# Kernel matrices and input projection of a state-space branch: from their own PSUM pools to the pool of the token projections

## The chip, the cores and the metric

One Trainium2 chip; the program runs on one of its cores. The metric is the device time of one execution in microseconds (us). Engines are called PE (TensorE, matmuls; PEld is its weight load), DVE (VectorE), ACT (ScalarE), POOL (GpSimd) and SP (SyncE, which issues most DMAs). "q0" and "q1" below are the two halves of the query projection.

## What is computed

A decoder block on 512 tokens of width 1024: RMS norm, one input projection (`w_in`), an S5 state-space branch and a sliding-window attention branch side by side, gates, an output projection, then a PEER mixer (128 experts for each token out of 16384). Only the front of it matters here:

```python
xn = rms_norm(h, ln1_g[layer])
proj = xn @ w_in[layer]
u_s5, q, k, v, gate_logits = jnp.split(proj, splits, axis=-1)
...
# s5_mixer: from the parameters alone
abar = exp(lam * step);  bbar = coef * b
# from the parameters and u_s5
h_t = abar * h_(t-1) + bbar @ u_t
y_t = c @ h_t + d * u_t
```

(`s5_mixer` is given here in short.) The kernel treats four tokens as one block. For that it builds from the parameters, for 16 sets of groups, a 128x128 kernel matrix `tt` of a block's inputs to its outputs, and the matrices `el` (input to state) and `f` (state to output).

## The kernel before, in words

**Pools of PSUM.** The eight banks are split in `run` (L1215 on): `psc` has two buffers with the tag "sc", `ptr` two with the tag "tr", `pmm` four with the tag "mm". A tile asks its pool for a buffer in the order in which the Python code makes the tiles, and a buffer that had an earlier tile is handed on when that tile's last reader is done.

**Token projections.** `proj_tok` takes all four buffers of `pmm` (tiles `tps`, one for each 128 tokens) and runs for k/v, q0 and q1 in turn: 96 matmuls each, three (L94, L95, L96) for every product, since each weight is split by ACT into `hi` (L124) and by DVE or POOL into `lo` (L125). The query tiles are read by ACT twice: `qt` (L549), which a DMA writes out as `q_d` (L553), and `sq` (L550), which has one buffer and is reduced by DVE into `ssq` (L551).

**Projection of the state space's input.** `proj_u` runs four times: 24 matmuls into one tile `ups` (L491, before the change from `psc`), then `ut` (L495, DVE), then copies into `up` (L500, DVE and ACT). Gate tiles `gps` come from `psc` too.

**The state space's parameters.** `s5_params` makes, on DVE and POOL, long rows of small complex products (L281 to L288) and a chain of squarings (L281 to L288 on 128x16, then L331 to L336; twelve instructions, called a turn below), whose results POOL turns into the tables `co` and `si`. Four times it then transposes two tables (`wtr`, L417, from `ptr`; read by ACT as `el`, L418), spreads a table into two tiles `wrep` (L422, ACT, one buffer each), runs eight matmuls into a tile `kps` (L419 and L426, before the change from `ptr`), and takes `kps` out in four additions by DVE (L432) and three copies by ACT (L434), which go to the same tile `tt` in turn. `s5_mix` then starts with the matmuls `eps` (L449, from `pmm`).

**Order.** `front` weaves the Python steps of the projections (k/v, q0, q1, `proj_u`) with those of `s5_params`. What each engine runs, and in which order, is then set by a scheduler which simulates the pools, engines and waits with its own costs. Each engine runs its own row of instructions in that order, so an instruction which waits holds all that stand behind it.

Of the kernel before, what the change touches and what calls it, by code (L numbers as in the profile page):

```python
# [10 lines left out]
F32 = mybir.dt.float32  # L11
# [8 lines left out]
T = 512  # L20
# [38 lines left out]
class Builder:  # L59
# [230 lines left out]
    def s5_params(self, P, tp, res):  # L290
# [107 lines left out]
        for gh in range(2):  # L398
            G = slice(8 * gh, 8 * gh + 8)
            bc = lambda a: a[:, G, None].to_broadcast(sh)  # L400
            fr, fi, cre, cim = f_re[:, G], f_im[:, G], c_re[:, G], c_im[:, G]
            self.cmul(tp, bb_re, bb_im, bc(cr), bc(ci), b_re[:, G], b_im[:, G], sh, "b")
            for t, src, k in ((w_re, bb_re, 3), (w_im, bb_im, 3), (fr, cre, 0), (fi, cim, 0)):
                for o, s in halves(t, k):
                    nc.scalar.copy(o, src[s])
            for k in (1, 2, 3):
                self.cmul(tp, halves(w_re, 3 - k), halves(w_im, 3 - k), bc(ar[k]), bc(ai[k]), bb_re, bb_im, sh, "b")
            yield 6.0
            for k in (1, 2, 3, 4):
                self.cmul(tp, halves(fr, k), halves(fi, k), bc(ar[k]), bc(ai[k]), cre, cim, sh, "f", nc.gpsimd)  # L410
            yield 4.0
            for g0 in range(0, 8, 4):
                GG = slice(8 * gh + g0, 8 * gh + g0 + 4)
                for src, dst in ((w_re, el[0]), (w_im, el[1])):
                    ps = self.ptr.tile([128, 4, 128], F32, tag="tr", name=self.nm("wtr"))
                    for g in range(4):
                        nc.tensor.transpose(ps[:, g, :], src[:, g0 + g].rearrange("p s g c -> p (s g c)"), self.ident)  # L417
                    nc.scalar.copy(dst[:, GG, :], ps)  # L418
                ps = self.ptr.tile([128, 4, 128], F32, tag="tr", name=self.nm("kps"))  # L419
                wr = [tp.tile([128, 4, 4, 32], F32, tag=f"wrep{i}", name=self.nm("wrep")) for i in range(2)]  # L420
                for i, (w, sign) in enumerate(((w_re, 1.0), (w_im, -1.0))):
                    nc.scalar.activation(wr[i], w[:, g0:g0 + 4, 3:4].rearrange("p a s g c -> p a s (g c)").to_broadcast(  # L422
                        [128, 4, 4, 32]), AF.Copy, scale=sign)
                for g in range(4):
                    for i, f in enumerate((fr, fi)):
                        nc.tensor.matmul(ps[:, g, :], wr[i][:, g].rearrange("p s c -> p (s c)"),  # L426
                                         f[:, g0 + g, 0:4].rearrange("p s g c -> p (s g c)"), start=(i == 0), stop=(i == 1))
                di = tp.tile([128, 4, 32], F32, tag="di", name=self.nm("di"))
                nc.vector.tensor_mul(di, i4[:, None, :].to_broadcast([128, 4, 32]), dsk[:, GG, None].to_broadcast([128, 4, 32]))
                for s in range(4):  # L430
                    q = slice(32 * s, 32 * s + 32)
                    nc.vector.tensor_add(tt[q, GG, 32 * s:32 * s + 32], ps[q, :, 0:32], di[q])  # L432
                    if s < 3:
                        nc.scalar.copy(tt[q, GG, 32 * s + 32:128], ps[q, :, 32:128 - 32 * s])  # L434
                yield 2.0
# [51 lines left out]
    def proj_u(self, xh, xl, up):  # L487
        nc = self.nc
        for kk in range(4):
            wh, wl = self.unit_cols(self.i["w_in"], kk * 128, 128)  # L490
            ps = self.psc.tile([128, T], F32, tag="sc", name=self.nm("ups"))  # L491
            for k in range(KD):
                self.mm3(ps, wh[:, k, :], wl[:, k, :], xh[:, k, :], xl[:, k, :], k == 0, k == KD - 1)
            ut = self.ep.tile([128, T], F32, tag="e2", name=self.nm("ut"), bufs=1)
            nc.vector.tensor_mul(ut, ps, self.rb)  # L495
            v = ut.rearrange("p (n s) -> p s n", s=4)
            for q in range(4):
                for s in range(4):
                    cp = nc.scalar.copy if s % 2 else nc.vector.tensor_copy
                    cp(up[32 * s:32 * s + 32, 4 * kk + q, :], v[32 * q:32 * q + 32, s, :])  # L500
            yield 5.2
# [982 lines left out]
```

## Time and profile before

| | |
|---|---|
| median of 3 runs | 1680.63 us (1680.52 to 1682.4) |
| the profiled execution | 1685.87 us, its span 1684.1 us |
| mean granted clock of TensorE | 0.988 |
| PE busy | 1616.7 us, 96% of the span |
| DVE busy | 1417.1 us, 84% |
| ACT busy | 836.0 us, 50% |
| POOL busy | 529.9 us, 31% |

The profile follows one execution. Its times count from the start of the span. A line such as `[3.55 <-DVE tt L432]` behind an instruction says that its engine sat idle for 3.55 us before it and that the last thing to come was DVE's instruction on `tt` at L432. All that the change names lies between 59 and 150 us, within the first tenth of the span.

### The profile page before, as it was taken

To read this page: it belongs to the slowest core of one execution; us is meant where nothing else is said; L and a number is where in the kernel's file an instruction comes from. 1 tells how busy PE (TensorE), PEld (TensorE's weight loads), DVE (VectorE), ACT (ScalarE), POOL (GpSimd) and SP (SyncE) were. 2 spreads that over 40 slices of the span, in tenths; PEclk is the share of its full clock that TensorE was granted. 3 is DMA by queue.
4 is the path that set the end of the run, shared out by engine and by line. 5 is a ranking of instruction groups with operands and counts; after the bars stand their busy time and mean duration, and the time that the engine had idled before them with its cause. 6 is when DMAs were issued, how large, how long until landed. Compare 5 with 4: busy or idle time off the path is not lost.

```text
span 1684.1 us, 25275 instructions
## 1 busy us (share of the span) xinstructions
PE 1616.7 (96%) x8831; PEld 1422.9 (84%) x8831; DVE 1417.1 (84%) x2931; ACT 836.0 (50%) x1290; POOL 529.9 (31%) x472
## 2 busy tenths in 40 slices
PE   7799999998999999999999999999999999999998
PEld 5577887786899999999999999888888887888887
DVE  7699868897797899999998976878788777878895
ACT  5256566565555346675776863333333333333332
POOL 2564022332631222222222223333333333343330
PEclk9899999999999999999999999999999999999999
DMA  7823352645764666877876989999999999999994
GB/s 233 157 88 95 113 181 92 196 139 159 222 183 138 213 241 239 302 275 254 292 271 235 342 304 348 316 335 341 328 358 343 330 345 333 340 343 354 330 361 155
DMA packets 236880, 430.42 MB, mean 256 GB/s; under 512 B 17440, under 2 KB 153680, under 8 KB 233680
## 3 DMA queue, kind: packets, MB, share of 16 engines
q1 hardware_dynamic: 174752, 241.12, 42.6%
q0 software_dynamic: 36864, 134.23, 22.6%
q10 hardware_dynamic: 25136, 53.45, 9.8%
q8 instruction: 69, 1.13, 0.3%
q14 instruction: 59, 0.48, 0.1%
HBM read 374.08 MB, written 54.66 MB: 255 GB/s over the span
## 4 chain that ended last, share of the span: by engine, by line
PE 58%; DVE 17%; DMA 5%; issue 4%; ACT 2%; POOL 0%; SPq 0%; DVEq 0%; ACTq 0%; POOLq 0%
PE po L1166 8%; PE po L1168 8%; PE po L1165 8%; PE pa L94 7%; PE pa L96 7%; PE pa L95 7%; DVE lo L125 4%; DMA v_a<-A_d 3%; DVE sp_row L1215 2%; PE pg L1092 1%; ACT hi L124 1%; PE pg L1093 1%; DMA gl<-g_d 1%; DVE g_oh L1110 1%; PE qps L94 1%
## 5 line engine op out<-in xcount | busy, mean ns | idle before, releaser
L125 DVE TENSOR_TENSOR lo<-t_raw,hi 128x1024 fp32r<-128x1024 f32 x256 | 313.1, 1223 | 59.5 <-ACT hi L124 57.3
L124 ACT CAST hi<-t_raw 128x1024 fp32r<-128x1024 f32 x256 | 268.1, 1051 | 181.1 <-PE pa L95 127.2
L94 PE MATMUL pa<-x2h,hi 128*128 128x384 f32 x1024 | 347.5, 339 | 8.1 <-ACT hi L124 6.1
L96 PE MATMUL pa<-x2h,lo 128*128 128x384 f32 x1024 | 344.7, 339 | 3.2 <-DVE lo L125 3.2
L95 PE MATMUL pa<-x2l,hi 128*128 128x384 f32 x1024 | 344.2, 336 | 0.0
L1198 POOL DMA_INDIRECT sp_row<-peer_u,sp_ei x128 | 177.5, 1386 | 446.3 <-DVE sp_row L1215 401.2
L1198 POOL DMA_INDIRECT sp_row<-peer_v,sp_ei x128 | 168.0, 1312 | 332.3 <-DVE sp_acc L1217 306.4
L1166 PE MATMUL po<-lo,v_wh 128*128 128x512 f32 x768 | 264.4, 395 | 1.7 <-DVE lo L125 1.7
L1168 PE MATMUL po<-hi,v_wl 128*128 128x512 f32 x768 | 241.2, 394 | 0.0
L1165 PE MATMUL po<-hi,v_wh 128*128 128x512 f32 x768 | 238.4, 395 | 0.9 <-ACT hi L124 0.7
L1155 ACT CAST v_wh<-v_w 128x384 fp32r<-128x384 f32 x128 | 65.8, 514 | 347.3 <-DVE v_w L1154 293.9
L94 PEld LDWEIGHTS pa<-x2h,hi 128*128 128x128 f32 x1024 | 193.2, 189 | 13.1 <-ACT hi L124 8.6
L96 PEld LDWEIGHTS pa<-x2h,lo 128*128 128x128 f32 x1024 | 192.9, 189 | 5.0 <-DVE lo L125 4.5
L95 PEld LDWEIGHTS pa<-x2l,hi 128*128 128x128 f32 x1024 | 193.0, 188 | 0.9
L1166 PEld LDWEIGHTS po<-lo,v_wh 128*128 128x128 f32 x768 | 143.6, 187 | 36.8 <-DVE lo L125 2.9
L1165 PEld LDWEIGHTS po<-hi,v_wh 128*128 128x128 f32 x768 | 143.4, 187 | 36.1 <-ACT hi L124 2.5
L1168 PEld LDWEIGHTS po<-hi,v_wl 128*128 128x128 f32 x768 | 143.9, 187 | 35.4
L1217 DVE SCALAR_TENSOR_TENSOR sp_acc<-sp_row,sp_a,sp_acc 128x1024 f32<-128x1024 f32 x128 | 163.9, 1280 | 0.4
L1215 DVE SCALAR_TENSOR_TENSOR sp_row<-sp_row,xrow 128x1024 f32<-128x1024 f32 x128 | 156.0, 1219 | 4.6 <-DMA sp_row<-peer_u,sp_ei 4.5
L124 ACT CAST hi<-raw 128x1024 fp32r<-128x1024 f32 x88 | 92.0, 1048 | 86.2 <-PE gps L95 15.6
L125 POOL TENSOR_TENSOR lo<-raw,hi 128x1024 fp32r<-128x1024 f32 x28 | 68.8, 2458 | 118.8 <-ACT hi L124 118.7
L1108 ACT COPY g_one<-g_o 128x1024 f16<-128x1024 f16 x48 | 99.1, 2065 | 7.7 <-DVE g_o L1107 5.3
(457 smaller groups left out, 2985.8 us busy)
## 6 DMA issues: line engine op xcount, KB each, us to landing
t_raw<-peer_uT SPq DMA_DIRECT2D x128, 512.0 KB, 4.6
t_raw<-peer_v SPq DMA_DIRECT2D x128, 512.0 KB, 7.0
G_d<-g_st ACTq DMA_DIRECT2D x24, 1024.0 KB, 6.4
v_g<-G_d SPq DMA_DIRECT2D x64, 384.0 KB, 9.4
raw<-w_in SPq DMA_DIRECT2D x32, 512.0 KB, 4.4
A_d<-u_g ACTq DMA_DIRECT2D x70, 192.0 KB, 4.1
v_a<-A_d SPq DMA_DIRECT2D x70, 192.0 KB, 8.4
raw<-w_ab SPq DMA_DIRECT2D x64, 128.0 KB, 3.3
```

Source lines behind the costliest of these rows:

```text
L94: mm(out, lh, rh, start=first, stop=False)
L95: mm(out, lh, rl, start=False, stop=False)
L96: mm(out, ll, rh, start=False, stop=last)
L124: self.nc.scalar.copy(hi, raw)
L125: (self.nc.gpsimd if pool_lo else self.nc.vector).tensor_sub(lo, raw, r32(hi))
L1108: nc.scalar.copy(one, o1.rearrange("p b t -> p t b"))
L1165: mm(po[j][i], wh[:, c], hi[:, hs[i]], start=first, stop=False)
L1166: mm(po[j][i], wh[:, c], lo[:, hs[i]], start=False, stop=False)
L1168: mm(po[j][i], wl[:, c], hi[:, hs[i]], start=False, stop=last)
L1198: nc.gpsimd.indirect_dma_start(out=got[k], out_offset=None, in_=self.i[n], in_offset=bass.IndirectOffsetOnAxis(ap=ei[:, s:s + 1], axis=0))
L1215: nc.vector.scalar_tensor_tensor(r, r, 1.0, xrow, op0=ALU.mult, op1=ALU.mult, accum_out=av[:, s:s + 1])
L1217: nc.vector.scalar_tensor_tensor(acc, r, av[:, s:s + 1], acc, op0=ALU.mult, op1=ALU.add)
```

## The change

Two tiles come from another pool: `kps` (four of them) from `pmm` in place of `ptr`, and `ups` (four) from `pmm` in place of `psc`. Nothing else in the code differs.

```diff
-                ps = self.ptr.tile([128, 4, 128], F32, tag="tr", name=self.nm("kps"))
+                ps = self.pmm.tile([128, 4, 128], F32, tag="mm", name=self.nm("kps"))
...
-            ps = self.psc.tile([128, T], F32, tag="sc", name=self.nm("ups"))
+            ps = self.pmm.tile([128, T], F32, tag="mm", name=self.nm("ups"))
```

In the order in which the code makes its tiles, the first two of the four `kps` stand between q0's four `tps` and q1's four. The last number of a name below counts the tiles as they are made: `tps_164_708` to `tps_167_711` are q0's tiles, `kps_262_1072` and `kps_279_1160` the first two kernel matrices, `tps_299_1236` to `tps_302_1239` q1's, `kps_327_1360` and `kps_336_1424` the last two, and then `ups_357_1517` and three more. With the change all of these go through the four buffers of `pmm` in that turn. The scheduler also makes other rows of instructions from it. Three places follow.

PE where q0 ends, as the difference between the two kernels ("+" is new at this place; six rows more of `kps_262_1072` stand where the dots are):

```order
 L96 MATMUL tps_167_711<-hi_267_1096,xl_115 128x512
+L426 MATMUL kps_262_1072<-f_re_879,wrep_263_1073 128x128
+L426 MATMUL kps_262_1072<-f_im_880,wrep_264_1074 128x128
...
+L426 MATMUL kps_279_1160<-f_re_879,wrep_280_1161 128x128
 L94 MATMUL tps_299_1236<-hi_304_1242,xh_114 128x512
 L95 MATMUL tps_299_1236<-lo_305_1243,xh_114 128x512
```

The first kernel matrix, which stood behind 76 of q1's 96 matmuls, and one matmul of the second, which stood behind all of them, now stand ahead of q1's first.

DVE around the splits of the last weights for q1 and the first for `ups`, before (`rn` is part of a turn of squarings):

```order
L334 TENSOR_SCALAR rn_103_517<-rn_103_517 128x16
L125 TENSOR_TENSOR lo_342_1449<-raw_340_1446,hi_341_1448 128x1024
L335 TENSOR_TENSOR sqr_97_505<-sqr_97_505,rn_103_517 128x16
L336 TENSOR_TENSOR sqi_98_506<-sqi_98_506,rn_103_517 128x16
L281 TENSOR_TENSOR cm1_107_527<-sqr_97_505 128x16
```

and with the change:

```order
L286 TENSOR_TENSOR sqr_137_605<-cm1_139_607,cm2_140_608 128x16
L125 TENSOR_TENSOR lo_342_1449<-raw_340_1446,hi_341_1448 128x1024
L288 TENSOR_TENSOR sqi_138_606<-cm3_141_609,cm4_142_610 128x16
...
L336 TENSOR_TENSOR sqi_146_626<-sqi_146_626,rn_151_637 128x16
L125 TENSOR_TENSOR lo_361_1563<-raw_359_1560,hi_360_1562 128x1024
L551 TENSOR_REDUCE ssq_94<-sq_344_1459 128x8
```

The split `lo_342_1449` stood in the turn that makes `rn_103`; it now stands in the turn that makes `sqr_137`, five turns further on. The first `ssq` of q1 stood inside the turn that makes `sqr_129`; it now stands behind the whole turn of `sqr_145`, two turns further on, and behind the split `lo_361_1563`.

PE where q1 ends and `ups` starts, before:

```order
L96 MATMUL tps_302_1239<-hi_341_1448,xl_115 128x512
L94 MATMUL ups_357_1517<-xh_114,hi_355_1513 128x512
L95 MATMUL ups_357_1517<-xl_115,hi_355_1513 128x512
L96 MATMUL ups_357_1517<-xh_114,lo_356_1514 128x512
L94 MATMUL ups_357_1517<-xh_114,hi_355_1513 128x512
L417 MATMUL wtr_278_1154<-ident_58,w_im_893 128x128 x4
```

and with the change (`ktr` are transposes of the keys, which stood behind the state space's mixing):

```order
L96 MATMUL tps_302_1239<-hi_341_1448,xl_115 128x512
L426 MATMUL kps_327_1360<-f_re_879,wrep_328_1361 128x128
...
L577 MATMUL ktr_458_2278<-ident_58,kv_120 128x128 x4
L577 MATMUL ktr_459_2291<-ident_58,kv_120 128x128 x4
L426 MATMUL kps_336_1424<-f_re_879,wrep_337_1425 128x128
L94 MATMUL ups_357_1517<-xh_114,hi_355_1513 128x512
L95 MATMUL ups_357_1517<-xl_115,hi_355_1513 128x512
```

Three of the four `kps` now stand whole ahead of `ups`, and of the last its first matmul; before, three stood among the matmuls of `ups` and of the gates.

## Rows read from the trace of the kernel before

**Rows 1.** The page, busy time of the span by engine: us, share, instructions.

```profile
PE 1616.7 (96%) x8831; PEld 1422.9 (84%) x8831; DVE 1417.1 (84%) x2931; ACT 836.0 (50%) x1290; POOL 529.9 (31%) x472
```

**Rows 2.** The waits of PE between 60 and 151 us: what it waited for, us in total, times, the longest.

```profile
PE kps L426 <- DVE tt L432: 5.5, 3, 3.5
PE tps L94 <- ACT sq L550: 3.2, 1, 3.2
PE ups L94 <- DVE ut L495: 2.4, 1, 2.4
```

**Rows 3.** Busy time of the engines by stretch (a table by windows): after the window and its length come PE, PEld, DVE, ACT and POOL busy us with their instructions, the granted clock, the DMA share and GB/s. Behind the part that the change touches; the last row sums 16 windows from 147.74 to 460 us.

```profile
147.74:160.00 12.26, 12.26 (x64) 10.45 (x63) 11.21 (x24) 5.52 (x8) 0.14 (x2) 1.00 0.42 129
...
180.00:200.00 20.00, 20.00 (x113) 17.36 (x113) 20.00 (x38) 9.59 (x27) 2.57 (x3) 1.00 0.35 100
...
sum 312.26, PE 295.43 PEld 250.39 DVE 255.13 ACT 181.90 POOL 84.37; mean PE 18.46 PEld 15.65 DVE 15.95 ACT 11.37 POOL 5.27
```

**Rows 4.** The timeline of PE where q0 ends and q1 starts: start, us, engine, line, operation, [idle time before it and who ended it].

```profile
62.69 0.79 PE L94 MATMUL tps<-hi,xh 128*128 128x512 f32 x1 [3.19 <-ACT sq L550]
```

**Rows 5.** The timeline of ACT before the first kernel matrix.

```profile
75.86 0.69 ACT L549 ACTIVATE qt<-tps,rx 128x512 f32<-128x512 f32 x1 [11.39 <-DMA q_d<-qt]
...
79.74 0.62 ACT L422 ACTIVATE wrep<-w_im 128x512 f32<-128x512 f32 x1
```

**Rows 6.** The timeline of PE, the first matmul of the first `kps` and what follows its last, then two matmuls of the third `kps`.

```profile
93.50 0.38 PE L426 MATMUL kps<-f_re,wrep 128*128 128x128 f32 x2
...
95.28 0.60 PE L417 MATMUL wtr<-ident,w_re 128*128 128x128 f32 x4
...
130.53 0.63 PE L426 MATMUL kps<-f_re,wrep 128*128 128x128 f32 x2
130.95 0.64 PE L426 MATMUL kps<-f_im,wrep 128*128 128x128 f32 x2
```

**Rows 7.** The timeline of DVE between 83 and 104 us.

```profile
83.46 0.17 DVE L286 TENSOR_TENSOR sqr<-cm,cm 128x16 f32<-128x16 f32 x1
...
84.23 0.28 DVE L283 TENSOR_TENSOR cm<-a3r,bb_im 128x128 f32<-128x128 f32 x1
84.42 0.29 DVE L284 TENSOR_TENSOR cm<-a3i,bb_re 128x128 f32<-128x128 f32 x1
...
88.39 0.17 DVE L281 TENSOR_TENSOR cm<-sqr 128x16 f32<-128x16 f32 x1
...
89.56 1.22 DVE L125 TENSOR_TENSOR lo<-raw,hi 128x1024 fp32r<-128x1024 f32 x1
...
90.90 0.17 DVE L281 TENSOR_TENSOR cm<-sqr 128x16 f32<-128x16 f32 x1
...
94.04 0.35 DVE L281 TENSOR_TENSOR cm<-sqr 128x16 f32<-128x16 f32 x1
...
97.78 0.17 DVE L281 TENSOR_TENSOR cm<-sqr 128x16 f32<-128x16 f32 x1
...
98.61 0.57 DVE L286 TENSOR_TENSOR w_re<-cm,cm 64x128 f32<-64x128 f32 x2
...
103.32 0.67 DVE L551 TENSOR_REDUCE ssq<-sq 128x8 f32<-128x512 f32 x1
```

**Rows 8.** All instructions on `kps`: duration in ns (least, median, most), first and last start; the additions that DVE takes it out with.

```profile
L432 DVE TENSOR_TENSOR tt<-kps,di x16: 270/286/296, 98.2 to 149.3; 32x128 f32<-32x128 f32 x16
```

**Rows 9.** Busy time by stretch, columns as in rows 3, of the part in question.

```profile
78.80:91.00 12.20, 12.20 (x50) 9.59 (x51) 11.95 (x58) 5.92 (x9) 0.00 (x0) 0.87 0.22 64
91.00:104.00 13.00, 13.00 (x70) 10.99 (x69) 12.67 (x56) 5.84 (x11) 12.15 (x31) 1.00 0.54 163
104.00:117.00 13.00, 10.52 (x56) 8.38 (x54) 12.69 (x43) 7.45 (x13) 7.20 (x11) 1.00 0.28 87
```

**Rows 10.** The timeline of ACT, q1's tail.

```profile
96.31 0.57 ACT L418 COPY el<-wtr 128x512 f32<-128x512 f32 x1
...
99.63 0.68 ACT L550 ACTIVATE sq<-tps,rx 128x512 f32<-128x512 f32 x1
...
105.18 1.04 ACT L124 CAST hi<-raw 128x1024 fp32r<-128x1024 f32 x1
```

**Rows 11.** The timeline of PE, the start of `ups`, the longest waits behind it, and the first `eps`.

```profile
100.39 0.40 PE L94 MATMUL ups<-xh,hi 128*128 128x512 f32 x1
100.62 0.39 PE L95 MATMUL ups<-xl,hi 128*128 128x512 f32 x1
...
118.05 0.50 PE L94 MATMUL ups<-xh,hi 128*128 128x512 f32 x1 [2.41 <-DVE ut L495]
...
129.22 0.46 PE L426 MATMUL kps<-f_re,wrep 128*128 128x128 f32 x2 [3.55 <-DVE tt L432]
...
147.74 1.95 PE L449 MATMUL eps<-up,el 128*128 128x128 f32 x16
```

**Rows 12.** Busy time by stretch, columns as in rows 3, two stretches of 3.5 and 4 us behind two of these waits.

```profile
119.50:123.00 3.50, 3.50 (x12) 2.77 (x11) 3.42 (x7) 2.43 (x6) 3.50 (x6) 0.51 0.00 0
...
129.20:133.20 4.00, 3.98 (x21) 4.00 (x22) 3.92 (x6) 3.75 (x7) 4.00 (x7) 0.58 0.00 0
```

**Rows 13.** All instructions on `ktr`, columns as in rows 8.

```profile
L577 PE MATMUL ktr<-ident,kv x8: 270/273/273, 201.7 to 202.4; 128*128 128x128 f32 x8
```

**Rows 14.** The timeline of POOL, one instruction of the tables.

```profile
103.24 0.43 POOL L283 TENSOR_TENSOR cm<-co,sqi 128x128 f32<-128x128 f32 x1
```

## The prediction

> **What bounds the kernel now.** I read the busy times first: PE is busy 1616.7 of 1684.1 us [rows 1], so that the time is PE's work plus the holes in it, and a change in waits is worth only what PE's holes lose or gain. Next the waits of PE in the part that the change touches: between 60 and 151 us it waited 3.2 us for ACT's `sq` (q0's last tiles), 5.5 us in three pieces for `kps` to get its bank back from DVE's additions, and 2.4 us for the bank of `ups` [rows 2]. The last two groups, 7.9 us, are what other banks can take away. Then the stretches behind: from 147.74 us on, where `eps` starts, PE is busy 12.26 of 12.26 us, and so it stays over 180 to 200, where DVE is busy 20.00 of 20 as well; from there to 460 us PE idles 312.26 - 295.43 = 16.8 us in all, none of it before 220 [rows 3]. A start of `eps` that moves by some us therefore moves what follows. The question is when `eps` starts: 147.74 in the profile [rows 11].
>
> **The first step: a kernel matrix ahead of q1.** The pools hand out buffers in the order of the code, and there the first two `kps` stand before q1's four tiles. With four buffers, q1's third and fourth tile get those of the first and second `kps`, and the scheduler has put the eight matmuls of the first, and one of the second, ahead of all of q1. PE can't start them when q0 is out, but only when ACT has both `wrep`, whose last one starts at 79.74 and takes 0.62 [rows 5]: 80.4. Until now PE used this hole: q0 ended at 62.69 - 3.19 = 59.5, and q1 started at 62.69 [rows 4]. Its matmuls of that time now lie behind. What stands ahead of that `wrep` on ACT is the same in both kernels, the wait of 11.39 us for the DMA of `q_d` among it [rows 5], so I let 80.4 stand. Eight `kps` matmuls took 95.28 - 93.50 = 1.78 us at the full clock, and 0.42 us each at the lower one [rows 6]; behind a hole of 20 us I take the lower, 3.4 us, so 83.8. The second pair of `wrep` has the same two buffers, so its first tile costs 0.62 more, and q1 starts at 84.6. Its 96 matmuls at 0.23 us (the step of two in rows 11) are 22.1 us, the second `kps` 1.8, some 2 us of `wtr` and a restart at the lower clock 1 to 2 more: q1 ends at 112, if nothing else holds it. I let it end at 115, since its last matmuls wait for `lo_342` and its fourth tile for the second `kps` to be taken out. Before it ended at 100.39 [rows 11]. So 14.7 us are lost here first. The third `kps` (1.8) and the transposes `ktr` (0.8, [rows 13]) follow at once, until 117.6. Work has moved ahead of `ups` which stood among it: three `kps` and `ktr`.
>
> **The second step: the last `kps` waits for ACT, ACT for DVE.** The last `kps` stands with one matmul at the head of `ups`. It needs its `wrep` and the banks that q1's second tile had; on ACT that `wrep` stands behind the whole tail of q1: `sq` of the second tile, which waits until DVE has reduced the first one (`sq` has one buffer), then `qt`, two `el`, `sq`, `hi`, `qt`, `sq`, `wrep`. At 0.68, 0.57 and 1.04 us for `sq` (and `qt`), `el` and `hi` [rows 10], and 0.62 for `wrep` [rows 5], these nine are 0.68 x 5 + 0.57 x 2 + 1.04 + 0.62 = 6.2 us when added up, and some 0.1 less for each since ACT starts the next a bit early: 5.7 us. So it hangs on the end of the first `ssq` of q1 on DVE.
>
> DVE has no hole there (12.67 of 13 and 12.69 of 13 us busy, [rows 9]), so its time is a sum. Up to 83.46 [rows 7] nothing has moved. There it now meets the first addition of the first `kps`, which comes out at 83.8 to 84.2: a wait of 0.7. Four additions at 0.29 [rows 8] and one `di` of 0.2 come in ahead of the turn that started at 88.39, and a `lo` goes out of it: it starts at 90.4. Instructions on DVE follow each other with an overlap of 84.23 + 0.28 - 84.42 = 0.09, so a `lo` of 1.22 costs 1.13. A turn with one `lo` in it took 90.90 - 88.39 = 2.51 us while POOL was idle, and 97.78 - 94.04 = 3.74 while POOL was at work [rows 7, 9]: 1.4 and 2.6 without the `lo`. So this turn ends at 91.8. Then follow, up to the end of that `ssq`, three `lo` (3.4), four additions (1.2), twelve halves of `w_re` and `w_im` at 0.30 (3.6, the row at 98.61 holds two), eight products of 128x128 at 0.2 (1.6), `di` 0.2 and `ssq` 0.6: 10.6 us [rows 7, 8], and six turns. All six at 1.4 end at 110.8, all at 2.6 at 118.0. POOL was busy 12.15 and 7.20 of 13 us in the two stretches behind 91 us [rows 9], and it now gets its inputs sooner, as the turns come sooner; so I take a value near the upper bound, 116.5.
>
> 116.5 + 5.7 = 122.2: the last `kps` and `ups` start there, 4.6 us after PE has run out of work.
>
> **The third step: `ups` without waits.** From there PE has four `ups` and one gate tile of 24 matmuls at 0.23, 5.55 each, and 1.8 of `kps`: 29.5 us. I see no wait in it: the four `ups` have buffers that q1 and the third and fourth `kps` left long before, and DVE has only `ut`, copies and `lo` there. So the 7.9 us go, as they should, and `eps` starts at 151.7. Behind the waits of 2.41 and 3.55 us the granted clock fell to 0.51 and 0.58, the lower level of 1.2 GHz, for 3.5 and 4 us of the work that followed [rows 11, 12]: 3.5 x 0.49 = 1.7 us each. The new hole of 4.6 us is of that kind. Since its length is the least sure number here, I put in 1.1 of the 1.7. Against that, `ktr`, 0.8 us, stood behind `eps` and is done by then. In all 151.7 + 1.1 - 0.8 - 147.74 = **4.3 us later**.
>
> The table of stretches has no hole of PE from 147.74 to 220 us [rows 3], so the shift goes on. The scheduler also reorders the attention behind; no row tells me a price for that, and I give it nothing, with 3 us to either side.
>
> **Sum.** The profiled execution took 1685.87 us, 1.8 us around its span among it; + 4.3 makes 1690.2. It lies 5.2 us above the median of the runs, 1680.63, and the shift is the same for both: **1685.0 us**.
>
> **Rivals.**
> (a) *The hole behind q1 stays short.* If turns cost DVE 1.4 rather than 2.6, `ssq` ends at 110.8, `lo_342` no longer holds q1, and `ups` starts when PE is ready, at 112 + 2.6 = 114.6, or after ACT, at 116.5. Then `eps` starts at 116.5 + 29.5 = 146.0, with no lowered clock, and with the 0.8 of `ktr` the kernel gains 2.5 us, up to 4.4 if ACT is not late either: 1677.3. For it speaks that POOL idled in part of the second stretch, against it that DVE gave POOL work in each turn.
> (b) *The shift is absorbed.* The 16.8 us of PE's holes from 220 to 460 us [rows 3] may not all hang on the chain that is late; where one waits for a DMA that was issued early, 4 us vanish. Then 1680 to 1683. Against it: DVE was full for 180 to 200, and what waits there for DVE waits later.
> (c) *DVE and POOL lock each other out.* In a turn that ran beside POOL the twelve instructions took 2.6 us in place of 1.4, so 0.1 us more for each, while one POOL instruction of the tables takes 0.43 us [rows 7, 14]. If each of the twelve waited for a whole one, a turn would cost 1.4 + 12 x 0.43 = 6.6 us, and five of the six turns would add 20 us to what I count at 2.6. As only a part of the turns meets a busy POOL, I put it at 13 us, 1698. The Trainium skill, "SBUF — State Buffer", section "Who interferes with whom", says that a VectorE instruction with two SBUF inputs and a GpSimd one that reads SBUF exclude each other for the whole instruction. The rows show them slowed, yet by a quarter of that; so I leave it a small chance.
>
> (d) *The banks pay in full.* If PE loses its 7.9 us of waits [rows 2] and the order costs nothing, since what stands behind `kps` at q1 is made up before `eps`, the kernel takes 1680.63 - 7.9 = 1672.7. The change says that the banks are free by then: for `ups` they are, for the first two `kps` they aren't, since q1 comes after them in the pool and PE is short of work from 59.5 on. So this has little for it. The Trainium skill, "Perfetto Trace Analysis", section "Matmuls", has it as a rule: independent groups of matmuls should rotate through different PSUM banks, so that one group is taken out while the next runs. By that rule the waits go; the trace has them, 7.9 us, and has no row for a loss beside them.
>
> **How the numbers follow.** A run of this kernel can be told from no change from about 0.2% on, 3.4 us. My forecast has 0.52, of which a fifth falls below 3.4 us; (a) 0.18, three quarters of it faster by more than 3.4 us when the clock and the attention's order help; (b) 0.21; (c) 0.06; (d) 0.03. Together: faster 0.14 + 0.03 = 0.17, same 0.10 + 0.04 + 0.20 = 0.34, slower 0.42 + 0.01 + 0.06 = 0.49. The range leaves out (c) and (d) and reaches from (a) with half a us to spare, 1676.5, to the forecast with all six turns at 2.6 (+1.5), the full price of the clock (+0.6) and 3 us of the attention, 1690.
>
> **What would show it.** Right: PE idle from 59.5 to about 80.4, then `kps` ahead of q1; q1's end near 115; a wait of 3 to 5 us ahead of the last `kps`, put down to ACT's `wrep` or `sq`; no wait for `ut` or `tt` inside `ups`; `eps` near 152, and the same shift at 200 us. Wrong: `wrep` much sooner than 80 us since the DMA of `q_d` lands earlier; `ups` starting by 117; an order of the attention that is worth more than 3 us by itself.

## The result and the profile after

The change makes the kernel slower: 1698.1 us (median of 4 runs, 1694.94 to 1698.33) against 1681.52 for the kernel before (4 runs), a ratio of 1.009 with a 95% interval of [1.0076, 1.0103]. A second measurement (`after2` below) gave 1698.14 against 1684.04, 1.0084 [1.0069, 1.0098]. So it costs 14 to 17 us; the forecast was 4.3, with an upper end of 1690.

The profiled execution took 1694.94 us, 9.1 more than the profiled one of before, since that one lay 4 above its median and this one 3 below. The two traces are therefore compared by when things start, up to 480 us; behind that they differ by what single executions differ.

The waits of PE between 60 and 160 us, where before had [rows 2]:

```profile
PE kps L426 <- ACT wrep L422: 23.4, 4, 19.7
PE ktr L577 <- ACT el L418: 3.8, 1, 3.8
PE wtr L417 <- DVE w_re L286: 1.7, 1, 1.7
PE tps L95 <- DVE lo L125: 1.5, 1, 1.5
PE tps L94 <- DVE tt L432: 0.2, 1, 0.2
```

Before, there is one wait more in this stretch than [rows 2] and the prediction list, and it is the longest: inside q1, PE waited for a `hi` which stands on ACT behind the same wait of 11.39 us for the DMA of `q_d` [rows 5]. The row of the waits of before, and the matmul that waited:

```profile
PE tps L94 <- ACT hi L124: 7.7, 1, 7.7
```

```profile
78.79 1.90 PE L94 MATMUL tps<-hi,xh 128*128 128x512 f32 x3 [7.67 <-ACT hi L124]
```

None of the waits of before is left, neither those of the banks (7.9 us, as the change means it) nor the others (3.2 and 7.7). In their place PE waits 23.4 us for `wrep`: 19.7 ahead of q1 and 3.1 ahead of the last `kps`, with 3.8 for `ktr` between. So the hole ahead of q1 is not all new: up to 79 us PE had stood still for 10.9 us before as well, and had done only some 8 us of q1 in between.

Busy time from the end of q0 to `eps`, columns as in [rows 3], before and with the change:

```profile
59.50:147.74 88.24, 69.52 (x314) 56.45 (x314) 74.82 (x240) 48.00 (x93) 60.32 (x113) 0.88 0.41 104
59.50:159.70 100.20, 69.46 (x322) 56.66 (x322) 74.20 (x243) 48.45 (x95) 57.88 (x116) 0.83 0.37 92
```

PE is busy for 69.5 us in both, and idle for 18.7 us before and 30.7 with the change. The 12.0 us by which `eps` is late are PE's idle time.

PE's timeline with the starts that answer to [rows 4, 6, 11]:

```profile
79.42 0.77 PE L426 MATMUL kps<-f_re,wrep 128*128 128x128 f32 x2 [19.70 <-ACT wrep L422]
...
84.58 0.77 PE L94 MATMUL tps<-hi,xh 128*128 128x512 f32 x1
...
117.01 0.38 PE L426 MATMUL kps<-f_re,wrep 128*128 128x128 f32 x2
...
122.80 1.60 PE L577 MATMUL ktr<-ident,kv 128*128 128x128 f32 x8 [3.84 <-ACT el L418]
127.52 0.80 PE L426 MATMUL kps<-f_re,wrep 128*128 128x128 f32 x2 [3.12 <-ACT wrep L422]
...
159.70 1.95 PE L449 MATMUL eps<-up,el 128*128 128x128 f32 x16
```

q1 starts at 84.58 in place of 62.69, `ups` behind the row at 127.52 in place of 100.39, and `eps` at 159.70 in place of 147.74: 12.0 us late. DVE's timeline up to q1's first reduction, where before had [rows 7]: the first instruction of a turn and of the one behind it, then the first of the last turn ahead of the reduction, the six in it that took long, and what follows.

```profile
90.54 0.17 DVE L281 TENSOR_TENSOR cm<-sqr 128x16 f32<-128x16 f32 x1
...
92.04 0.17 DVE L281 TENSOR_TENSOR cm<-sqr 128x16 f32<-128x16 f32 x1
...
114.79 0.17 DVE L281 TENSOR_TENSOR cm<-sqr 128x16 f32<-128x16 f32 x1
...
114.97 0.60 DVE L283 TENSOR_TENSOR cm<-sqr,sqi 128x16 f32<-128x16 f32 x1
...
115.57 0.59 DVE L286 TENSOR_TENSOR sqr<-cm,cm 128x16 f32<-128x16 f32 x1
...
116.20 0.56 DVE L331 TENSOR_TENSOR rn<-sqr 128x16 f32<-128x16 f32 x1
...
116.88 0.48 DVE L333 TENSOR_TENSOR rn<-rn,rn 128x16 f32<-128x16 f32 x1
117.39 0.65 DVE L334 TENSOR_SCALAR rn<-rn 128x16 f32<-128x16 f32 x1
118.08 0.65 DVE L335 TENSOR_TENSOR sqr<-sqr,rn 128x16 f32<-128x16 f32 x1
118.65 0.16 DVE L336 TENSOR_TENSOR sqi<-sqi,rn 128x16 f32<-128x16 f32 x1
118.73 1.64 DVE L125 TENSOR_TENSOR lo<-raw,hi 128x1024 fp32r<-128x1024 f32 x1
120.30 0.67 DVE L551 TENSOR_REDUCE ssq<-sq 128x8 f32<-128x512 f32 x1
```

The turn from 90.54 takes 1.50 us, with POOL idle; the one from 114.79 takes 118.73 - 114.79 = 3.94. Six of its twelve instructions, which take 0.16 to 0.18 us each in the turn from 90.54, take 0.48 to 0.65 there. POOL was in its products of 128x256 then, this one among them:

```profile
117.97 0.72 POOL L288 TENSOR_TENSOR si<-cm,cm 128x256 f32<-128x256 f32 x1
```

ACT's timeline behind that reduction, where before had [rows 10]:

```profile
121.00 0.69 ACT L550 ACTIVATE sq<-tps,rx 128x512 f32<-128x512 f32 x1 [6.77 <-DVE ssq L551]
...
123.10 0.72 ACT L550 ACTIVATE sq<-tps,rx 128x512 f32<-128x512 f32 x1
...
125.68 0.69 ACT L549 ACTIVATE qt<-tps,rx 128x512 f32<-128x512 f32 x1 [0.93 <-DMA q_d<-qt]
126.27 0.68 ACT L550 ACTIVATE sq<-tps,rx 128x512 f32<-128x512 f32 x1
126.84 0.63 ACT L422 ACTIVATE wrep<-w_re 128x512 f32<-128x512 f32 x1
```

ACT stands 6.77 us until DVE has reduced `sq`, and the `wrep` of the last `kps` is out at 127.47. The row at 123.10 reads q1's third tile for the last time: its bank is that of the first `ups`, and is free from 123.8 on. `ups` starts at 127.97, right behind the matmul of the last `kps` at 127.52, which stands ahead of it in PE's row.

### The profile page after: what moved, and what is told of

Its sections match the earlier page's. It is cut to its first block, busy times and chain, and to the rows that moved or that the text cites. A ratio compares the mean times of both kernels' runs of the same rounds, so it can differ in the third digit from the quotient of the medians.

```text
span 1693.2 us, 25275 instructions
## 1 busy us (share of the span) xinstructions
PE 1614.5 (95%) x8831; PEld 1425.0 (84%) x8831; DVE 1417.7 (84%) x2931; ACT 837.0 (49%) x1290; POOL 526.2 (31%) x472
## 4 chain that ended last, share of the span: by engine, by line
PE 66%; DVE 8%; DMA 2%; issue 1%; ACT 1%; POOL 0%; SPq 0%; DVEq 0%; ACTq 0%; POOLq 0%
PE po L1166 11%; PE po L1165 11%; PE po L1168 11%; PE pa L94 9%; PE pa L96 9%; PE pa L95 9%; DVE lo L125 2%; PE pg L1092 1%; PE pg L1093 1%; DVE sp_row L1215 1%; PE ops L1166 1%; PE ops L1168 1%; PE ops L1165 1%; ACT hi L124 1%; PE qps L94 1%
```

## The experiments

Theory A says that the first two `kps` ahead of q1 are the loss. The rivals put it on `ups`, on the attention's order, or on DVE's contention with POOL. Times are medians; each is compared with runs of the kernel before on the same chip. "eps" is the first start of `eps` in the run's trace, which is one execution; the two traces of the changed kernel (159.7 and 159.0) differ by 0.7 us.

### Which half costs: e1_kps, e2_ups, e3_late, e15_ups_split, after2

e1_kps has only the first of the two edited lines of the change, e2_ups only the second. e3_late has the second and, for `kps` (`gh` is 0 for the first two; the diff is against the kernel before):

```diff
-                ps = self.ptr.tile([128, 4, 128], F32, tag="tr", name=self.nm("kps"))
+                ps = (self.pmm if gh else self.ptr).tile([128, 4, 128], F32, tag="mm" if gh else "tr", name=self.nm("kps"))
```

e15_ups_split has the first and, for `ups`, again against the kernel before:

```diff
-            ps = self.psc.tile([128, T], F32, tag="sc", name=self.nm("ups"))
+            ps = (self.psc if kk < 2 else self.pmm).tile([128, T], F32, tag="sc" if kk < 2 else "mm", name=self.nm("ups"))
```

> The change for the kernel matrices alone; ups stays in its old pool. PE has q0, the first kps, q1 in the same order as with the whole change, ups has two buffers of its own, and the attention behind 200 us stands almost as before the change. Theory A (the first two kps ahead of q1 cost it): PE idles from 59.5 to about 79.5, the first reduction of q1 ends near 120 on DVE, eps starts at 155 to 160, and the time is 1692 to 1699 us. Rival B (the loss comes from ups in the other pool and from the order of the attention): no more than 1685 us. Rival C (both halves cost about alike): 1688 to 1691 us.

> The change for ups alone; kps stays in its old pool, and q1 starts at 62.7 us as before. Theory A: the wait of 2.4 us for the bank of ups goes, with at most the 1.7 us of the lowered clock behind it, and no other: eps at 144 to 147.7, the time 1677 to 1682 us. Rival B: slower, 1688 us or more. Rival C: 1688 to 1691 us.

> The change, but with the first two kps left in their old pool, so that q1's four tiles come first in the pool and only the last two kps and ups use the four buffers. Theory A: q1 starts at 62.7 us and ends near 100, the waits of 3.55 and 2.41 us go for a part, eps at 142 to 148, the time 1674 to 1683 us. Rival B (it is ups and the kps of the second half that cost): 1688 us or more.

> The change, but the first two ups in their old pool and only the last two in the four buffers. Theory U (the half of the loss that is not the early kps is that the first ups stands behind q1's third and fourth tile in the pool, and these are taken out late): ups starts at 117 to 119 us, straight behind the third kps, eps at 152 to 155, the time 1685 to 1691 us. Rival V (it is the two last ups, or the kps of the second half, that wait for banks): ups starts at 122 or later, eps at 157 to 160, 1693 us or more.

> The whole change once more, on the chip of the three runs beside it, as their reference. Eps at 159 to 160.5 us, the time 1694 to 1700 us, 0.7 to 1.0% above the kernel before.

| run | us | ratio to before, 95% | eps | first `qps` |
|---|---|---|---|---|
| e1_kps | 1688.48 | 1.003 [1.0018, 1.0043] | 153.6 | 471.3 |
| e2_ups | 1685.73 | 1.0014 [1.0003, 1.0025] | 150.7 | 468.7 |
| e3_late | 1681.81 | 0.9996 [0.9985, 1.0007] | 146.1 | 465.1 |
| e15_ups_split | 1688.44 | 1.0028 [1.0018, 1.0037] | 152.4 | 472.0 |
| after2 (the whole change) | 1698.14 | 1.0084 [1.0069, 1.0098] | 159.0 | 479.9 |
| before (its profile) | | | 147.7 | 467.0 |

The early `kps` alone cost 5 us, which is what rival C gave for them and less than theory A wanted (1692 to 1699); what A said of PE's hole (19.8 us) and of DVE's reduction (its end at 120.5) held. `ups` alone costs 2.3 us, outside A's range and below C's. Together they cost 14: the halves don't add up, which none of these theories had (at the upper ends of their intervals they come to 11.4 us, and the whole change costs 11.6 at the lower end of its own; at eps 5.9 + 3.0 = 8.9, where the whole change has 11.3 to 12.0). PE's timeline of e1_kps at the point where the whole change has its two holes (the last matmuls of the third `kps` are followed by the first `ups`):

```profile
118.05 0.39 PE L426 MATMUL kps<-f_im,wrep 128*128 128x128 f32 x2
118.19 0.47 PE L94 MATMUL ups<-xh,hi 128*128 128x512 f32 x1
...
127.10 0.80 PE L426 MATMUL kps<-f_re,wrep 128*128 128x128 f32 x2 [2.94 <-ACT wrep L422]
...
153.63 1.95 PE L449 MATMUL eps<-up,el 128*128 128x128 f32 x16
```

The `wrep` of the last `kps` is as late as with the whole change (127.10 against 127.52), but PE does `ups` from 118.19 on meanwhile, as it has a bank of its own. With the whole change that bank is q1's third tile, which ACT reads until 123.8, and the scheduler has put `ups` behind the first matmul of the last `kps`, which waits for that `wrep` until 127.5. e15_ups_split gives just the first two `ups` their old bank back: `ups` stands ahead of the last `kps` again and starts at 118.0, and the time is that of e1_kps, as theory U said. In e3_late q1's tiles come first in the pool; its q1 starts at 62.8, and the time can't be told from before. A wait of 6.0 us for ACT's `el` stands there for the waits that went. e2_ups has one of 8.0 us for the same reason:

```profile
PE kps L426 <- ACT el L418: 8.0, 1, 8.0
```

### POOL's products: e5_nopool, e6_before_nopool

```diff
-                G = slice(g, g + step)
-                self.cmul(tp, co[:, G, m:2 * m], si[:, G, m:2 * m], co[:, G, 0:m], si[:, G, 0:m],
+                G = slice(g, g + step); cm = self.cmul if m < 16 else lambda _, o, i, *r: ([self.nm("cm") for _ in range(4)], nc.gpsimd.memset(o, 1.0), nc.gpsimd.memset(i, 0.0))
+                cm(tp, co[:, G, m:2 * m], si[:, G, m:2 * m], co[:, G, 0:m], si[:, G, 0:m],
```

The first is made on the whole change, the second on the kernel before. Both leave out a part of the work: those parts of `co` and `si` are constants.

> The whole change, with the last three doublings of the tables co and si left out: POOL's 42 products of 128x256, which lie between 108 and 139 us, become fills with a constant without an input, at the start. PE, DVE and ACT run the same instructions in the same order as with the whole change. Theory D (DVE's row up to q1's first reduction ends at 120.9 rather than 116.5 because its two-input instructions stand against POOL's): that reduction ends at 113 to 117, eps starts 4 to 8 us earlier than 159.7, and the time is 1689 to 1694 us. Rival E (the sum on DVE was simply short by some us, POOL has no part): the reduction stays at 120 to 121, and the time at 1697 to 1699 us.

> The kernel before, with the last three doublings of the tables co and si left out in the same way as in e5_nopool; PE, DVE and ACT run the same instructions in the same order as the kernel before. Theory D (POOL's products stretch DVE's row, and it hurts the changed kernel more, as its first reduction of q1 and all of ups hang on that row): eps at most 3 us earlier than 147.7 and the time at most 0.2% below that of the kernel before. Rival: the products cost both kernels alike, so that this one gains as e5_nopool gained over the whole change, 6 us.

e5_nopool: 1691.76 us, 1.0054 [1.004, 1.0068], eps 155.8, 6 us less than the whole change. Its DVE timeline, the same turn as the one of 3.94 us above:

```profile
113.26 0.17 DVE L281 TENSOR_TENSOR cm<-sqr 128x16 f32<-128x16 f32 x1
...
114.56 0.17 DVE L335 TENSOR_TENSOR sqr<-sqr,rn 128x16 f32<-128x16 f32 x1
114.65 0.17 DVE L336 TENSOR_TENSOR sqi<-sqi,rn 128x16 f32<-128x16 f32 x1
114.74 1.22 DVE L125 TENSOR_TENSOR lo<-raw,hi 128x1024 fp32r<-128x1024 f32 x1
115.87 0.68 DVE L551 TENSOR_REDUCE ssq<-sq 128x8 f32<-128x512 f32 x1
```

1.48 us for the turn, and the reduction ends at 116.5 in place of 120.9: POOL's products do stretch DVE's row. The same row from the start of the turn before, with three `lo`, to the end of that reduction takes 7.0 us here (109.55 to 116.55) and 12.6 with the whole change (108.33 to 120.97). But e6_before_nopool gained as much: 1674.88 us, 0.9962 [0.995, 0.9975], eps 140.1, 7.6 earlier than 147.7. So the second clause of theory D falls. POOL's products are a price that both kernels pay; without them the change costs 15.7 us at eps (155.8 against 140.1), no less than with them.

### The tail of q1 and the hole ahead of it: e7_sq, e7b_tail, e8_qt, e10_late_both

On the whole change, e7_sq gives `sq` two more buffers, from the pool of `s5_params`:

```diff
-                sq = ep.tile([128, 512], F32, tag="e2", name=self.nm("sq"), bufs=1)
+                sq = self.tp.tile([128, 512], F32, tag="sqq", name=self.nm("sq"), bufs=2) if j in (1, 2) else ep.tile([128, 512], F32, tag="e2", name=self.nm("sq"), bufs=1)
...
-                bias_src = self.bias_table(tp, dp)
+                self.tp = tp; bias_src = self.bias_table(tp, dp)
```

and e8_qt, with the same second edit, gives `qt` two:

```diff
-                qt = ep.tile([128, 512], F32, tag="e1", name=self.nm("qt"))
+                qt = self.tp.tile([128, 512], F32, tag="qtq", name=self.nm("qt"), bufs=2) if j > 1 else ep.tile([128, 512], F32, tag="e1", name=self.nm("qt"))
```

e7b_tail has one more of each, used in q1 alone (`g and j % 2` for `sq`, `g and j == 2` for `qt`); e10_late_both is e3_late with one more of each (`j % 2`, `j == 2`).

> The whole change, with two more buffers for sq (for the second and third tile of each half of the queries), so that ACT need not wait for DVE's reduction before it takes out the next tile; PE's order is nearly the same as with the change. Theory F (the second step of the prediction: the last kps and ups wait for ACT's tail of q1, and that for DVE's first reduction): ACT's wait of 6.8 us is gone, the waits of 3.84 and 3.12 us ahead of ktr and of the last kps shrink to under 3 us in all, eps starts at 153 to 156, the time falls by 4 to 7 us to 1691 to 1694. Rival G (ACT's tail is late by what stands ahead of it, the splits of weights on DVE and PE's end of q1): eps stays at 158 to 160, 1696 us or more.

> The whole change, with one more buffer for sq and one more for qt in q1 alone, so that ACT's tail of q1 waits neither for DVE's reduction nor for the DMA of q_d; the hole ahead of q1 stays. Theory F (ups and the last kps wait for that tail): the waits on PE ahead of ktr and the last kps, 7.0 us with the change and 8.6 us in e7_sq, shrink to under 4 us, eps at 152 to 157, the time 1689 to 1694 us. Rival G (the tail is late by itself): eps at 158 to 160, 1696 us or more.

> The whole change, with two more buffers for qt (third and fourth tile of each half of the queries), so that ACT does not wait 11.3 us for the DMA of q_d ahead of the first wrep; the first kps still stands ahead of q1 on PE. Theory A (the hole of PE until the first wrep is the price of having kps ahead of q1): the hole of 19.7 us shrinks to 8 to 14, the first kps starts at 68 to 74, eps at 150 to 155, the time 1688 to 1694 us. Rival H (the hole is given back anyway, as DVE's row up to q1's first reduction is what counts, and it does not start sooner): eps 158 to 160, 1696 us or more.

> As e3_late (q1's tiles first in the pool, the last two kps and ups in the four buffers), with one more buffer each for sq and for qt. If the waits of ACT on the DMA of q_d and on the reductions set the time of the kernel before too: q1 starts without the wait of 7.4 us, ends near 93, eps at 134 to 142, the time 1668 to 1677 us. If other waits take their place (raw weights by DMA, DVE's row): eps at 144 or later, 1679 us or more.

e7_sq missed: 1699.98 us, 1.0102 [1.0087, 1.0117], eps 158.3. ACT's wait on DVE is gone, and another stands in its place, for the DMA that empties `qt`:

```profile
112.97 0.68 ACT L550 ACTIVATE sq<-tps,rx 128x512 f32<-128x512 f32 x1
122.83 0.69 ACT L549 ACTIVATE qt<-tps,rx 128x512 f32<-128x512 f32 x1 [8.22 <-DMA q_d<-qt]
```

e7b_tail, which frees `qt` as well, has 3.3 us of waits ahead of `ktr` and the last `kps` where the whole change has 7.0 (5.3 in after2), eps at 156.8 and 1695.87 us, 1.0071 [1.0055, 1.0086]: 2.2 us less than after2 by eps and by the median. That is theory F by the waits and eps, and less than it by the time, where the two intervals overlap. One wait of 3.4 us on a reduction was left, so the tail is not fully freed.

e8_qt is theory A's other test. The first `wrep` no longer stands behind the DMA of `q_d`, and the first `kps` starts ten us earlier:

```profile
69.39 0.77 PE L426 MATMUL kps<-f_re,wrep 128*128 128x128 f32 x2 [9.84 <-ACT wrep L422]
```

Eps goes to 147.9 and the time to 1687.85 us, 1.003 [1.0019, 1.0041], 10 us less than with the change. So the hole was a true price, but it is not all of these 11.8 us at eps: q1 starts at 78.1, 6.5 us sooner. The buffers also serve q1's tail, where ACT has no wait for the DMA left and waits 1.48 us for `ssq` in place of 6.77; `ups`, which stands behind the last `kps` here too, starts at 118.8 after a wait of 1.46. Yet eps is where it was before the change, and the kernel is 5 us slower: from eps to the first `qps` it takes 474.1 - 147.9 = 326.2 us, against 319.3 before; PE's waits there sum to 25.6 us, 16.9 before. The scheduler's order of the attention, to which the forecast gave nothing, is a likely cause of these 7 us, not a shown one; with the change itself (480.4 - 159.7 = 320.7) they are 1.4.

e10_late_both is 1681.69 us, 0.9997 [0.9986, 1.0008]. PE's wait of 7.4 us for `hi` is gone, but ACT still stands 10.69 us for the DMA of `q_d`, now at q0's fourth tile, and PE waits 6.6 us for the `sq` behind it and 7.1 us for `tt`; eps 144.9, 1.2 earlier than in e3_late. So extra buffers for `sq` and `qt` are worth little where no `kps` stands ahead of q1.

### DVE's row: e20_after_turns, e18_before_turns, e19_late_turns, e17_late_act

The first three have the turns of squarings on POOL, on the whole change, the kernel before and e3_late; the five lines behind the first one shown are changed in the same way:

```diff
-            nc.vector.tensor_mul(a, zr, zr)
+            nc.gpsimd.tensor_mul(a, zr, zr)
...
-            self.cmul(tp, a, b, zr, zi, zr, zi, [128, 16], "a")
+            self.cmul(tp, a, b, zr, zi, zr, zi, [128, 16], "z", nc.gpsimd)
```

e17_late_act is e3_late with

```diff
-                    cp = nc.scalar.copy if s % 2 else nc.vector.tensor_copy
+                    cp = nc.scalar.copy if s else nc.vector.tensor_copy
```

> The whole change, with the seven turns of squarings on POOL in place of DVE (84 small instructions and the six of the first squaring). Theory W (DVE's row is what q1's tail and, through the banks, ups hang on, and turns beside POOL cost it up to 3.9 us each): q1's first reduction ends by 108 to 113 rather than 120.9, ups starts at 116 to 121 rather than 127.5, eps at 147 to 153, the time 1684 to 1692 us. Rival X (PE's own row sets it: q1 starts at 84 us and its work cannot end before 112 to 115, so ups stays late): eps at 155 to 159, 1693 us or more.

> The kernel before with the seven turns of squarings on POOL. Theory W: DVE's row loses some 18 us of its 70 between 79 and 150, the waits of 5.5 us for kps and 2.4 us for ups go for the most part, eps at 138 to 143 us, the time 1672 to 1679 us. If PE's or ACT's own work or the tables on POOL, which then start later, take over: eps 144 to 148, 1680 us or more.

> As e3_late, with the seven turns of squarings on POOL: the late banks and the lighter row of DVE together. Theory W: eps at 136 to 142, the time 1669 to 1678 us, at or below that of e18_before_turns. If the banks are worth nothing once DVE is free: the same as e18_before_turns within 2 us.

> As e3_late, with three of four copies from ut to up on ACT and one on DVE (two and two before), since DVE is full from 79 to 147 us and ACT is not. If DVE's row sets when eps starts: eps at 140 to 144, the time 1674 to 1679 us. If PE's own work or ACT's takes over: eps at 145 to 148, 1680 to 1684 us.

e20_after_turns shows what q1's tail hung on. Its first reduction of q1 ends at 109.0 in place of 120.9, PE has no wait between 85 and 144, though `ups` stands behind the first matmul of the last `kps` there as well, and eps starts at 144.3, 15 us earlier than with the change and earlier than theory W asked. So PE's own row (rival X) did not hold it. The time is 1695.43 us all the same, 1.0068 [1.0048, 1.0087]: POOL, with the turns on top, finishes `si` at 160.9, and what was won is waited for there. DVE's waits of that run from 121 to 200 us, and PE's timeline:

```profile
DVE m L453 <- POOL si L288: 13.5, 1, 13.5
```

```profile
144.31 1.95 PE L449 MATMUL eps<-up,el 128*128 128x128 f32 x16
...
162.94 2.05 PE L449 MATMUL eps<-up,el 128*128 128x128 f32 x8 [4.56 <-DVE m L455]
```

e18_before_turns does the same to the kernel before: eps 135.5, then 9.1 us of PE's wait for `m`, and 1685.9 us, 1.0016 [1.0003, 1.003]. e19_late_turns took 1694.15 us, 1.0064 [1.0043, 1.0085]; its eps is at 139.5 and its first `qps` at 479.1, 339.6 us behind, 20.3 more than before; 12.8 of these lie in the mixing (53.0 us from the first to the last `eps`, 40.2 before), the rest behind it, in an attention that the scheduler ordered anew. e17_late_act took 1686.14 us, 1.0019 [1.0009, 1.0029]: eps at 145.4, but the mixing takes 45.6 us from the first to the last `eps` there; that ACT has the copies now is a likely cause, not a shown one. Against the kernel that each was made on, a lighter DVE brought eps forward by 15, 12 and 7 us in the first three and by 0.7 in the last, which is no more than two traces of one kernel differ by; the time did not follow. No version that does the whole work beats the kernel before by more than can be told from no change.

## Why the prediction was wrong

The direction was right, and so was the order of events; the size was not, 4.3 us in place of 14 to 17. By its steps, in the profiled execution:

**The first step held.** The first `kps` at 79.42 (80.4 forecast), q1 at 84.58 (84.6), q1's end at 117.0 (115), behind waits of 1.7 us for `w_re` and 1.5 for `lo`. These 2 us did not count, as PE then had to wait for ACT in any case. One reading in it was wrong: PE did not use the whole of this hole before, but stood still for 10.9 us of it. What the edit of `kps` costs by itself is in e1_kps: 5.9 us at eps, 5 us of time. That is what the whole forecast came to.

**The second step failed in DVE's sum.** It had q1's first reduction end at 116.5, 118.0 at most; it ended at 120.9. The term that was too small is the price of a turn beside POOL: 2.6 us, taken from a turn that ran beside POOL's smaller products, where the turns behind 108 us run beside those of 128x256 and take up to 3.94. For the last two turns, their three `lo` and the reduction the forecast had 2 x 2.6 + 3.4 + 0.6 = 9.2 us; they took 12.6. With these products left out they take 7.0, the last turn takes 1.48, and the reduction ends at 116.5; that this is the forecast's figure is chance, since the forecast had POOL at work in it. This is the mechanism of rival (c), which the forecast put aside, by half: six of a turn's twelve instructions last nearly as long as one product of POOL (0.65 beside 0.72), the others run at their own 0.16 to 0.17. The Trainium skill's rule that it named there ("SBUF — State Buffer", section "Who interferes with whom") fits these rows better than those of [rows 7], on which it was given a small chance; it speaks of two inputs, and the instruction at 117.39, which has one, took 0.65 as well. Rival (c)'s time of 1698 came out, but not by its cause: e6_before_nopool shows that the kernel before pays this price too. ACT's chain behind it took 6.6 us (to 127.5) for 5.7, of which 0.93 is a wait for the DMA of `q_d`.

**The third step failed in a sentence.** It said that the four `ups` have buffers which q1 left long before. The first has the bank of q1's third tile, read until 123.8. By itself this changes nothing in the sum, since `ups` stands behind the last `kps` in PE's row and could not start before 127.5 by that alone; between them, bank and place leave PE nothing to do from 119.0 to 127.5 but `ktr`. The forecast had 4.6 us of this hole, since it put `ups` behind the last `kps`, and did not see that this place cost anything against a kernel whose `ups` has its own bank. e1_kps and e15_ups_split against after2 show it: 9.7 us of the 14, of which 5.4 to 6.6 are there at eps. In the main these are the same us as those of the second step, seen from the other end: the hole goes when `ups` need not wait for the tail (e15_ups_split), and when the tail is early (e20_after_turns). From 127.52 to eps PE took 32.2 us, for 29.5 + 1.1; the clock was at its lower level, 0.50, up to 131.5, and at 0.70 to 135:

```profile
127.50:131.50 4.00, 3.98 (x10) 3.24 (x11) 3.46 (x10) 1.61 (x5) 4.00 (x7) 0.50 0.58 170
131.50:135.00 3.50, 3.50 (x12) 2.78 (x11) 0.86 (x2) 0.00 (x0) 3.50 (x7) 0.70 0.00 0
```

These are 7.5 us, so 4 x 0.50 + 3.5 x 0.30 = 3.1 us of loss for a term of 1.1 (two holes in a row stood ahead, not one).

Sum at eps: 4.4 (DVE) + 0.9 (ACT) + 1.6 (PE) on top of the forecast's 152.8 gives 159.7. The 0.8 us for `ktr` did not come back: eps to `qps` took 1.4 us more, not 0.8 less.

**What stays open.** Of after2's 14.1 us, 11.3 are there at eps and 12.9 at `qps`; the rest lies in the PEER stage, where single executions of one kernel differ by as much, and wasn't traced to a place. Between after2 and e15_ups_split there are 6.6 us at eps and 9.7 in the time; what makes the other 3 was not tried, beyond e8_qt, in which the same stretch took 7 more; at the first `qps` 7.9 are there. Each of these edits changes the banks and the scheduler's rows together; no run has the banks of one kernel with the rows of the other, so that the two prices are not told apart.

**The rivals.** (a) and (d) fell; the 7.9 us of waits went, as (d) said, and cost more elsewhere. (b) fell: nothing was absorbed between 220 and 460 us, the delay was 12.0 at eps and 13.4 at `qps`. In (a), 1677.3 is the middle of its two ends, 1678.1 and 1676.2, and the lower one lies outside the stated range; nothing hung on it.

## What to carry to other kernels

A pool that hands out buffers in program order makes a tile wait for all that stand before it there: ask of each tile that is moved into it whose bank it gets and when the last reader of that bank runs, and ask the same of the tiles that now come behind it. Two moves that cost 5 and 2 us alone cost 14 together, since one made a tail late and the other tied the next work to that tail. When the changed kernel is walked by hand, walk the one before in the same way and subtract, since a price that is too low (here DVE beside POOL) is then too low on both sides; setting a walk against a trace put the whole error into the difference. (The kernel before was not walked here, so this is advice and not a result.) And list all waits of a stretch: with the longest one left out, the holes of the two kernels differ by 19.5 us, with it by the 12.0 that eps shows.

## What the runs showed of the hardware

An instruction of DVE on 128x16 with two inputs, 0.17 us by itself, lasts up to 0.71 us beside POOL's products of 128x256 (0.61 to 0.74 us each where DVE's `lo` does not hold them); without them the same turn of twelve takes 1.48 us rather than 3.94. It goes the other way too: beside DVE's `lo` of 118.73 (1.64 us, 1.22 by itself) one such product takes 1.59 us:

```profile
119.25 1.59 POOL L282 TENSOR_TENSOR cm<-si,sqi 128x256 f32<-128x256 f32 x1
```

Leaving 42 such products out was worth 8 us to the kernel before (0.9962). POOL is busy for 31% of that kernel's span, but for 29.2 of the 40 us from 107 to 147, where these products lie.
